# Block-diagonal inverses kept in DRAM as their 32x32 blocks, and the first weight splits and beta casts tied behind the input's work: one core of a Trainium2 chip

## The chip, the cores and the metric

The kernel runs on one core of a Trainium2 chip. The metric is the device time of one execution in microseconds (us); the time before is the median of three runs, 2675.2 us (2672.99 to 2676.81). TensorE is called PE, VectorE DVE, ScalarE ACT, GpSimd POOL and SyncE SP; SP only issues DMAs.

## What is computed

One layer of a hybrid decoder in float32 on 2048 prompt tokens (D = 1024) and 64 sample tokens (8 sequences of 8). Cut to what matters here:

```python
u = rms_norm(x, norm_pre)
z = einsum('btd,de->bte', u, w_in)           # w_in is 1024 x 8208
lru_x, lru_gate, gdn_qkv, gdn_gate, gdn_b, gdn_a, m_lru, m_gdn = split(z)
h, lru_h = rg_lru(conv(lru_x), ...)          # a linear recurrence
q, k, v = split(silu(conv(gdn_qkv)))         # 8 heads of 128
beta, g = sigmoid(gdn_b), -exp(A_log) * softplus(gdn_a + dt_bias)
# gated delta rule, chunk by chunk: M is strictly lower triangular
Tinv = inverse(I + M)                        # M from k, beta and g
u_, w_ = Tinv @ (v*beta), Tinv @ (k*beta*exp(gc))
...                                          # state S carried from chunk to chunk
merged = sigmoid(m_lru)*(lru_out @ w_br_lru) + sigmoid(m_gdn)*(gdn_out @ w_br_gdn)
x_new = x + rms_norm(merged @ w_out, norm_post)
```

The outputs are the new x of both batches and the states.

## The kernel before

The prompt is worked off in four **blocks** of 512 tokens (block 0 has the 64 sample tokens too). A block has these stages, each a Python loop that emits code: the K projections of the 8 heads with the Gram matrices of the chunks (`t_gram`), the LRU's projections with the inverses of the diagonal blocks beside them (`t_inv`), the gated-delta stage with Q, V and gate projections of the 8 heads (`t_inv2`, `t_q`, `t_v`, `t_chain`), the branch products and the output product. A projection (`proj`, lines 551, 553, 555) multiplies a 1024 x 128 slice of weights with the 512 tokens. Both are split into a rounded high and a low part (`split`, line 205 for the low part), so each product is three matmuls.

**Weights.** Block 0 reads each raw slice from `w_in` and the other matrices (`wload`: tiles `raws`, two buffers, and `raw`, pairs of slices), splits it on ACT (high part, line 143) and DVE (low part, line 205) into a tile `whl`, and stores the split pair to DRAM (`dW`, 1 MB, line 279). Blocks 1 to 3 read `dW` back (line 300). `whl` has three buffers, so in block 0 a split waits until an earlier pair's store has landed.

**The order of work.** PE executes in the order in which the code is emitted: a small planner (`Weave`) steps generators in between the matmuls of the projections. DVE, ACT, POOL and SP are ordered by the framework's scheduler. `keep_in_program_order(x)` ties an instruction behind what its engine was given before it in the program. All engines execute in order. SP's DMAs use eight semaphores in turn, so a DMA of SP waits until the eighth before it has landed.

**The start.** `u_load` and `u_norm` read the first 512 + 64 tokens and normalise them; `u_tile`, eight times, has PE transpose a slice (line 196), ACT round it (tile `a`, line 143) and DVE take the low part (line 358). Then `wst`, the beta and decay columns of `w_in`, is cast (lines 431 to 433) and multiplied first (line 192, 32 matmuls), then come the small constants and the projections.

**The inverses.** A chunk has 128 tokens; `t_gram` stores its 128 x 128 matrix to `dM`. `t_inv` loads the 32 x 32 diagonal blocks of all 32 chunks and heads, one block to a partition (`Mb`, line 836), inverts them on DVE and stores the inverse and its transpose into the diagonal blocks of `dD` and `dDT`, 128 x 128 for each chunk, by 8 DMAs of 32 partitions (lines 848, 849), whose pieces in DRAM have 128 bytes. The rest of `dD` and `dDT` is zero: `t_zero` writes it in block 0 by 16 DMAs of 256 KB (line 504, pieces of 512 bytes). For each head, `t_inv2` loads `dM` (`Mt`, line 990), `dD` (`Dn`, one buffer, line 991) and `dDT` (`R`, two buffers, line 992), 4 chunks of 128 x 128 each. PE multiplies `Mt` with `Dn`, and in three steps fills in the blocks of `R` above the diagonal, which DVE writes (line 1008). `R` is then what `t_chain` uses.

```python
SP.dma_start(Dn, dD[hc].rearrange("c j i -> j c i"))
SP.dma_start(R, dDT[hc].rearrange("c j i -> j c i"))
```

Of the kernel before, what the change touches and what calls it, by code (L numbers as in the profile page):

```python
# [22 lines left out]
F32 = mybir.dt.float32  # L23
# [11 lines left out]
NCH = TB // 128  # L35
SB = 0
NS = 64
H = 8
# [116 lines left out]
def body(ctx, tc, x_prompt, x_sample, state_lru_conv, state_lru_h, state_gdn_conv, state_gdn_S,  # L155
# [47 lines left out]
    def split(hi, lo, src, eng=None):  # L203
        r = A.activation(hi, src, AF.Copy)
        (eng or G).tensor_tensor(out=lo, in0=src, in1=hi.bitcast(F32), op=OP.subtract)  # L205
        return r
# [36 lines left out]
    wlast = [None]  # L243
# [37 lines left out]
    def wfetch(ahead):  # L281

        while wnext[0] < len(worder) and len(wready) < ahead:
            n = wnext[0]
            e = worder[n]
            place = wplace[key(e)]
            out = isinstance(e[1], tuple)
            hl = wtile()
            hi, lo = (hl[:, j].rearrange("p (k c) -> p k c", c=256 if out else 128) for j in range(2))
            if n < len(wplace):  # L290
                while lnext[0] < len(wplace) and lnext[0] <= n + (
                        2 if paired[0] <= lnext[0] < paired[1] else 1):
                    wload(lnext[0])
                    lnext[0] += 1
                wstore(1)
                wlast[0] = split(hi, lo, wraws[key(e)], V)
                wstores.append((place, hl))
            else:
                wstore()
                SP.dma_start(hl.bitcast(F32), dW[place])  # L300
            wready.append((hi, lo))
            wnext[0] += 1
# [81 lines left out]

    dk = dram.tile([H, 128, TB + NS], F32, name="dk")
    dM = dram.tile([H * NCH, 128, 128], F32, name="dM")
    dD = dram.tile([H * NCH, 128, 128], F32, name="dD")
    dDT = dram.tile([H * NCH, 128, 128], F32, name="dDT")
    dE = dram.tile([H, 128, TB], F32, name="dE")
    dtm = dram.tile([16, 128, TB + NS], F32, name="dtm")  # L390
    dgc = dram.tile([H * NCH, 128], F32, name="dgc")
# [20 lines left out]
    with tc.tile_pool(name="init", bufs=2, side="right") as ip:  # L412
        with tc.tile_pool(name="u0", bufs=1) as up:
            r0 = ip.tile([8, 128], F32, name="r0")
            SP.dma_start(r0, rows(norm_pre))
            xh = u_load(0, up)
            t = gtile()
            tr(t[:, :8], r0, ident[:8, :8])
            V.tensor_copy(npre, t[:, :8])
            wraw = ip.tile([128, 8, 16], F32, name="wraw", bufs=1)  # L420
            SP.dma_start(wraw, win[:, C_B:C_B + 16].rearrange("(k p) c -> p k c", p=128))
            u_norm(xh, up)
            for n in range(2):
                wload(n)
                lnext[0] += 1
            SP.dma_start(dtb, bass.AP(tensor=gdn_dt_bias.tensor, offset=gdn_dt_bias.offset, ap=[[0, 128], [1, 8]]))
            SP.dma_start(negA, bass.AP(tensor=gdn_A_log.tensor, offset=gdn_A_log.offset, ap=[[0, 128], [1, 8]]))
            u = [u_tile(xh, k) for k in range(8)]
            zz = ip.tile([128, 96], F32, name="zz", bufs=1)
            V.memset(zz, 0.0)  # L430
            V.tensor_copy(wst[:, 256:352], zz)
            V.tensor_copy(wst3[:, :, 0:16], wraw)
            V.tensor_tensor(out=wst3[:, :, 16:32], in0=wraw, in1=wst3[:, :, 0:16].bitcast(F32), op=OP.subtract)
            wfetch(2)
        G.affine_select(out=tri, in_=ones, pattern=[[1, 128]], compare_op=OP.is_ge, fill=0.0,
                        base=0, channel_multiplier=-1)
        G.affine_select(out=offm.rearrange("p (a b) -> p a b", b=32), in_=ones.rearrange("p (a b) -> p a b", b=32),
                        pattern=[[-32, 4], [0, 32]], compare_op=OP.is_ge, fill=0.0, base=-32,
                        channel_multiplier=1)
        V.tensor_scalar(offm, offm, -1.0, None, op0=OP.mult)  # L440

        blk = const.tile([64, 64], F32, name="blk")
        blk3 = blk.rearrange("p (a b) -> p a b", b=8)
        G.affine_select(out=blk3, in_=ones[:64, :64].rearrange("p (a b) -> p a b", b=8),
                        pattern=[[-8, 8], [0, 8]], compare_op=OP.is_ge, fill=0.0, base=0, channel_multiplier=1)
        G.affine_select(out=blk3, in_=blk3, pattern=[[8, 8], [0, 8]], compare_op=OP.is_ge, fill=0.0,
                        base=7, channel_multiplier=-1)
        tris = const.tile([64, 64], F32, name="tris")
        V.tensor_tensor(out=tris, in0=blk, in1=tri[:64, :64], op=OP.mult)
        negs = const.tile([64, 64], F32, name="negs")  # L450
        V.tensor_scalar(negs, tris, 1.0, BIG, op0=OP.subtract, op1=OP.mult)
        bsel = blk3[:, :, 0]
        G.memset(halog, 0.0)
        G.memset(halol, 0.0)
        G.memset(hlast, 0.0)
        tc.keep_in_program_order(A.activation(negA, negA, AF.Exp))
        V.tensor_scalar(negA, negA, -1.0, None, op0=OP.mult)
# [39 lines left out]
    def t_zero(pool):  # L497

        z = pool.tile([128, 4, 128], F32, name="lru7")
        G.memset(z, 0.0)  # L500
        for h in range(H):
            yield 7000.0
            for dst in (dD, dDT):
                SP.dma_start(dst[4 * h:4 * h + 4].rearrange("c i j -> i c j"), z)
        yield 7000.0
        SP.dma_start(dDs.rearrange("h i j -> i h j"),
                     z[:64].rearrange("p a b -> p (a b)").rearrange("p (a b) -> p a b", b=64))
        zeroed[0] = True
# [22 lines left out]
    for blkno in range(NBLK):  # L531
# [299 lines left out]
        def t_inv():  # L831
            yield lambda: all(kdone)
            Mb = kl.tile([128, 32, 32], F32, name="Mb", tag="Mbinv", bufs=1)
            for b in range(4):
                q = slice(32 * b, 32 * b + 32)
                SP.dma_start(Mb[q], dM[:, q, q])
            if sb:
                Mbs = kl.tile([64, 8, 8], F32, name="Mbs", tag="Mbinvs", bufs=1)
                for b in range(8):
                    q = slice(8 * b, 8 * b + 8)  # L840
                    SP.dma_start(Mbs[q], dMs[:, q, q])
            yield 3000.0
            r = []
            yield from tri_inverse(kl, 32, 128, Mb, "inv", r)
            yield lambda: zeroed[0]
            for b in range(4):
                q = slice(32 * b, 32 * b + 32)
                SP.dma_start(dD[:, q, q], r[0][q])
                SP.dma_start(dDT[:, q, q], r[1][q])
            yield T_IN  # L850
            invdone[0] = True
            if sb:
                r = []
                yield from tri_inverse(kl, 8, 64, Mbs, "invs", r)
                for b in range(8):
                    q = slice(8 * b, 8 * b + 8)
                    SP.dma_start(dDs[:, q, q], r[1][q])
# [121 lines left out]
        def h2t(nm, bufs=B2, shape=None):  # L979
            return h2.tile(shape or [128, NCH, 128], F32, name=nm, tag=nm, bufs=bufs)  # L980

        def t_inv2(h):

            d = st_[h]
            hc = slice(NCH * h, NCH * h + NCH)
            d["kT"] = h2t("kT", B2, [128, NB])
            SP.dma_start(d["kT"], dk[h, :, :NB])
            Mt, Dn = h2t("Mt", 1), h2t("Dn", 1)
            R = d["R"] = h2t("R")
            SP.dma_start(Mt, dM[hc].rearrange("c j i -> j c i"))  # L990
            SP.dma_start(Dn, dD[hc].rearrange("c j i -> j c i"))
            SP.dma_start(R, dDT[hc].rearrange("c j i -> j c i"))
            d["Ed"] = h2t("Ed")
            SP.dma_start(d["Ed"], dE[h].rearrange("p (c i) -> p c i", c=NCH))
            d["loaded"] = True
            yield T_I2 if h else T_I20
            yield lambda: invdone[0]
            t = g3()
            for c in range(NCH):
                mm(t[:, c], Mt[:, c], Dn[:, c])  # L1000
            V.tensor_tensor(out=Mt, in0=t, in1=bc(offm[:, None, :], [128, NCH, 128]), op=OP.mult)
            for a in (2, 1, 0):
                yield T_NEU
                rows, cols = slice(32 * a, 32 * a + 32), slice(32 * a + 32, 128)
                t = g3()
                for c in range(NCH):
                    mm(t[rows, c, cols], Mt[:, c, rows], R[:, c, cols], cost=54.0 * (3 - a))
                V.tensor_copy(R[rows, :, cols], t[rows, :, cols])
            d["inv"] = True
# [343 lines left out]
```

## Time and profile before

| | us |
|---|---|
| median of three runs | 2675.2 |
| lowest and highest of them | 2672.99, 2676.81 |
| profiled execution, its own time | 2665.83 |
| its span | 2664.1 |
| PE busy in the span | 2564.3 (96%) |
| mean granted clock of PE | 0.991 of full speed |

The profile is of one execution. "Busy" is time in which an engine executes; what an engine waits for is given as idle time with its releaser. The granted clock is a share of 2.4 GHz: a stretch at 1.00 ran at 2.4 GHz throughout, one at less ran at 1.2 GHz for some of its time. A view by stretches gives busy times, the clock and the share of time for which the 16 DMA engines were occupied (the modelled ends can make it slightly over 1).

### The profile page before, as it was taken

The numbers are of one execution on the slowest core, as the hardware profiler recorded it, in microseconds if no ns is written. First come the engines' busy times: TensorE is split into PE (matmuls) and PEld (weight loads), VectorE is DVE, ScalarE is ACT, GpSimd is POOL, SyncE is SP. The second block draws the span as 40 slices with busy tenths as digits, with TensorE's granted clock in tenths as the row PEclk, the third lists the DMA queues.
The fourth block names the chain that finished last, engine by engine and source line by source line (L and its number), as shares of the span: only waits on it lengthen the run. The fifth ranks groups of instructions, "written<-read, shape, count | busy, mean of one in ns | idle before, by whom it ended". The sixth has DMA issues, their size and how long they took to land.

```text
span 2664.1 us, 39927 instructions
## 1 busy us (share of the span) xinstructions
PE 2564.3 (96%) x15332; PEld 2232.2 (84%) x15332; DVE 1508.0 (57%) x3521; ACT 886.9 (33%) x1722; POOL 378.0 (14%) x364
## 2 busy tenths in 40 slices
PE   6988889998999999999999999999999999999999
PEld 5888888887999788888889888888889888888888
DVE  4668668776544457566513457566513457566512
ACT  5336533333333235333303235333303235333301
POOL 0220111001210111110200211110211211100210
PEclk9999999999999999999999999999999999999999
DMA  7997988788877786544466886644466886545465
GB/s 210 253 285 181 261 202 202 181 173 162 307 269 270 256 271 217 203 168 164 158 240 255 273 275 213 208 162 167 158 237 256 272 277 214 202 169 168 160 236 201
DMA packets 327897, 581.82 MB, mean 218 GB/s; under 512 B 70849, under 2 KB 236762, under 8 KB 282650
## 3 DMA queue, kind: packets, MB, share of 16 engines
q1 hardware_dynamic: 313882, 553.57, 66.6%
q10 hardware_dynamic: 13824, 25.70, 2.6%
q8 instruction: 121, 1.98, 0.3%
q14 instruction: 70, 0.57, 0.1%
HBM read 421.61 MB, written 157.59 MB: 217 GB/s over the span
## 4 chain that ended last, share of the span: by engine, by line
PE 77%; DMA 10%; DVE 6%; issue 2%; ACT 2%; SPq 1%; POOL 1%; ACTq 0%; POOLq 0%; DVEq 0%
PE mm L555 18%; PE mm L553 18%; PE mm L551 18%; PE g L192 8%; PE c L192 5%; PE g L196 2%; PE mm L1294 2%; PE mm L1296 2%; PE mm L1298 2%; DMA er<-dgc 2%; DMA raws<-in_w_in_dram 2%; DMA dW<-whl 2%; DVE cvy L582 1%; DVE whl L205 1%; DMA dE<-er 1%
## 5 line engine op out<-in xcount | busy, mean ns | idle before, releaser
L551 PE MATMUL mm<-a,whl 128*128 128x512 f32 (+2 forms) x2432 | 862.3, 355 | 15.6 <-ACT tmo L143 11.9
L555 PE MATMUL mm<-a,whl 128*128 128x512 f32 (+2 forms) x2432 | 867.4, 357 | 7.3 <-DVE whl L205 7.3
L553 PE MATMUL mm<-a,whl 128*128 128x512 f32 (+2 forms) x2432 | 862.1, 354 | 0.0
L551 PEld LDWEIGHTS mm<-a,whl 128*128 128x128 f32 x2432 | 464.7, 191 | 64.0 <-ACT tmo L143 12.7
L555 PEld LDWEIGHTS mm<-a,whl 128*128 128x128 f32 x2432 | 464.7, 191 | 60.8 <-DVE whl L205 8.3
L553 PEld LDWEIGHTS mm<-a,whl 128*128 128x128 f32 x2432 | 464.6, 191 | 45.5
L582 DVE SCALAR_TENSOR_TENSOR cvy<-cvr,cwg,cvy 128x512 f32<-128x512 f32 x288 | 217.4, 755 | 17.9 <-ACT cvy L143 12.5
L553 PE MATMUL mm<-a,whx 128*128 128x512 f32 x448 | 181.7, 406 | 0.0
L555 PE MATMUL mm<-a,whx 128*128 128x512 f32 x448 | 181.4, 405 | 0.0
L551 PE MATMUL mm<-a,whx 128*128 128x512 f32 x448 | 179.3, 400 | 0.0
L1232 DVE SCALAR_TENSOR_TENSOR pt<-tm,mm 128x512 f32<-128x512 f32 (+1 forms) x80 | 47.3, 592 | 180.7 <-PE mm L555 180.6
L143 ACT ACTIVATE cvr<-mm 128x512 f32<-128x512 f32 (+1 forms) x160 | 81.6, 510 | 186.9 <-PE mm L555 179.1
L1086 POOL TENSOR_TENSOR st<-st,mhalf 128x4 f32<-128x4 f32 x32 | 38.9, 1215 | 653.4 <-DVE st L1084 653.4
L1294 PE MATMUL mm<-whl,bt 128*128 128x256 f32 x448 | 126.2, 282 | 1.2 <-DVE y L1303 1.2
L1298 PE MATMUL mm<-whl,bt 128*128 128x256 f32 x448 | 126.2, 282 | 0.2 <-DVE yss L1272 0.2
L1296 PE MATMUL mm<-whl,bt 128*128 128x256 f32 x448 | 126.3, 282 | 0.0
L143 ACT ACTIVATE yv<-c 128x128 f32<-128x128 f32 x128 | 35.5, 277 | 245.9 <-PE c L192 245.4
L143 ACT ACTIVATE th<-cvy 128x512 f32<-128x512 f32 (+1 forms) x96 | 61.9, 645 | 156.4 <-DVE cvy L582 130.9
L555 PE MATMUL mm<-gp,whl 128*128 128x512 f32 (+2 forms) x296 | 104.2, 352 | 0.0
L551 PE MATMUL mm<-gp,whl 128*128 128x512 f32 (+2 forms) x296 | 104.1, 352 | 0.0
L553 PE MATMUL mm<-gp,whl 128*128 128x512 f32 (+2 forms) x296 | 104.0, 351 | 0.0
L551 PEld LDWEIGHTS mm<-a,whx 128*128 128x128 f32 x448 | 84.5, 189 | 17.6
(341 smaller groups left out, 4476.1 us busy)
## 6 DMA issues: line engine op xcount, KB each, us to landing
whl<-dW SPq DMA_DIRECT2D x199, 1024.0 KB
dW<-whl SPq DMA_DIRECT2D x88, 1024.0 KB
whx<-dW SPq DMA_DIRECT2D x65, 1024.0 KB
raws<-in_w_in_dram SPq DMA_DIRECT2D x33, 512.0 KB
raw<-in_w_in_dram SPq DMA_DIRECT2D x15, 1024.0 KB
dtm<-tmo ACTq DMA_DIRECT2D x48, 256.0 KB
tm<-dtm SPq DMA_DIRECT2D x48, 256.0 KB
ux<-in_x_prompt_dram SPq DMA_DIRECT2D x16, 512.0 KB
```

Source lines behind the costliest of these rows:

```text
L143: r = f(*args, **kw)
L192: T.matmul(out, a, b, start=start, stop=stop)
L196: T.transpose(out, in_, idn)
L551: T.matmul(ps[:, :n], wh, mh[:, c0:c0 + n], start=k == 0, stop=False)
L553: T.matmul(ps[:, :n], wh, ml[:, c0:c0 + n], start=False, stop=False)
L555: T.matmul(ps[:, :n], lo[:, k, :], mh[:, c0:c0 + n], start=False, stop=k == 7)
L582: V.scalar_tensor_tensor(out=y[:, :TB], in0=raw[:, i:i + TB], scalar=cw[:, i, ti:ti + 1], in1=y[:, :TB], op0=OP.mult, op1=OP.add)
L1086: G.tensor_tensor(out=st[:, 3], in0=st[:, 2], in1=mhalf[:, :NCH], op=OP.pow)
L1232: proj(mov, lambda ps, c0, n: V.scalar_tensor_tensor(out=t_[:, c0:c0 + n], in0=x[:, c0:c0 + n], scalar=1.0, in1=ps[:, :n], op0=OP.add, op1 ...
L1294: T.matmul(ps[:, :256], mh[:, cs], wh[:, k % 4], start=k == 0, stop=False)
L1296: T.matmul(ps[:, :256], mh[:, cs], wl[:, k % 4], start=False, stop=False)
L1298: T.matmul(ps[:, :256], ml[:, cs], wh[:, k % 4], start=False, stop=k == 7)
```

## The change

```diff
@@ wfetch
                 wlast[0] = split(hi, lo, wraws[key(e)], V)
+                if n < 4:
+                    tc.keep_in_program_order(wlast[0])
@@
-    dD = dram.tile([H * NCH, 128, 128], F32, name="dD")
-    dDT = dram.tile([H * NCH, 128, 128], F32, name="dDT")
+    dD = dram.tile([4, H * NCH, 32, 32], F32, name="dD")
+    dDT = dram.tile([4, H * NCH, 32, 32], F32, name="dDT")
@@ the start
-            V.memset(zz, 0.0)
+            tc.keep_in_program_order(V.memset(zz, 0.0))
             V.tensor_copy(wst[:, 256:352], zz)
-            V.tensor_copy(wst3[:, :, 0:16], wraw)
+            tc.keep_in_program_order(V.tensor_copy(wst3[:, :, 0:16], wraw))
@@ t_zero
-        G.memset(z, 0.0)
-        for h in range(H):
-            yield 7000.0
-            for dst in (dD, dDT):
-                SP.dma_start(dst[4 * h:4 * h + 4].rearrange("c i j -> i c j"), z)
+        G.memset(z[:64], 0.0)
@@ t_inv
-            for b in range(4):
-                q = slice(32 * b, 32 * b + 32)
-                SP.dma_start(dD[:, q, q], r[0][q])
-                SP.dma_start(dDT[:, q, q], r[1][q])
+            for dst, m in ((dD, r[0]), (dDT, r[1])):
+                SP.dma_start(dst.rearrange("b n i j -> (b n) i j"), m)
@@ before t_inv2, once for each block
+        blkd = []
+        for i in range(3):
+            blkd.append(h2.tile([128, NCH, 128], F32, name=f"blkd{i}"))
+            G.memset(blkd[i], 0.0)
@@ t_inv2
-            Mt, Dn = h2t("Mt", 1), h2t("Dn", 1)
-            R = d["R"] = h2t("R")
+            Mt, Dn = h2t("Mt", 1), blkd[2]
+            R = d["R"] = blkd[h % 2]
             SP.dma_start(Mt, dM[hc].rearrange("c j i -> j c i"))
-            SP.dma_start(Dn, dD[hc].rearrange("c j i -> j c i"))
-            SP.dma_start(R, dDT[hc].rearrange("c j i -> j c i"))
+            for b in range(4):
+                q = slice(32 * b, 32 * b + 32)
+                SP.dma_start(Dn[q, :, q], dD[b, hc].rearrange("c i j -> i c j"))
+                SP.dma_start(R[q, :, q], dDT[b, hc].rearrange("c i j -> i c j"))
```

`dD` and `dDT` now hold only the diagonal blocks. The 16 DMAs of zeros are gone; each block's 8 stores of inverses become 2, of 128 partitions with pieces of 4 KB; each head's two loads become 8 of 32 partitions (pieces of 128 bytes) into tiles that POOL has set to zero once in the block. The first four splits on ACT, and on DVE the zero columns and the first cast of `wst`, are tied behind what their engines were given before.

ACT at the start: `whl<-raws` is the high part of a weight split, `a<-g,npre` the rounding of a transposed slice of the input, 512 columns for the prompt and 64 for the samples. Two pieces of the difference:

```order
 L143 ACTIVATE ux_216<-ux_216,urr 128x1024
-L143 ACTIVATE whl<-raws 128x1024
-L143 ACTIVATE a<-g,npre 128x512
-L143 ACTIVATE a<-g,npre 128x64
-L143 ACTIVATE whl<-raws 128x1024
-L143 ACTIVATE a<-g,npre 128x512
-L143 ACTIVATE a<-g,npre 128x64
-L143 ACTIVATE negA<-negA 128x8
-L143 ACTIVATE a<-g,npre 128x512
-L143 ACTIVATE a<-g,npre 128x64
-L143 ACTIVATE whl<-raws 128x1024
```

```order
+L143 ACTIVATE a<-g,npre 128x512
+L143 ACTIVATE a<-g,npre 128x64
+L143 ACTIVATE whl<-raws 128x1024 x2
+L143 ACTIVATE negA<-negA 128x8
 L143 ACTIVATE zr<-mm 32x256
 L143 ACTIVATE zr<-mm 32x320
```

The three splits that stood between the roundings are gone from there; two stand behind the eighth pair, and the third and the fourth further down, behind the Tanh of the first K projection (`th`). On DVE, the low parts of the first two and the casts of `wst` stand behind the eight low parts of the input too.

SP a little later, first before, then changed: `raws` and `raw` are raw weights, `dW` a store of a split pair, `dD<-lru` and `dDT<-lru` the first zeros.

```order
L473 DMA er<-in_state_lru_h_dram 64x128
L265 DMA raws<-in_w_in_dram 128x8x128
L271 DMA raw<-in_w_in_dram 128x8x256
L279 DMA dW_80<-whl 128x2048
L271 DMA raw<-in_w_in_dram 128x8x256
L279 DMA dW_81<-whl 128x2048
L279 DMA dW_82<-whl 128x2048
L504 DMA dD<-lru_870 128x4x128
L504 DMA dDT<-lru_870 128x4x128
```

```order
L475 DMA er<-in_state_lru_h_dram 64x128
L271 DMA raw<-in_w_in_dram 128x8x256 x2
L265 DMA raws<-in_w_in_dram 128x8x128 x2
L279 DMA dW_80<-whl 128x2048
L279 DMA dW_81<-whl 128x2048
L504 DMA dDs<-lru_870 64x8x64
L271 DMA raw<-in_w_in_dram 128x8x256
```

The third raw slice, which was loaded among the constants, now comes with the fourth, behind the loads of slices 4 to 7. Further on, two more `raws`, of the slices that are used around 310 us, stand some 20 and 35 DMAs behind these rows; before, they came behind the inverses' stores.

POOL and SP at the start of the gated-delta stage of block 1, changed (before, the three rows of `blkd` were not there, and SP had one `Dn` and one `R` in place of the eight loads). `lru<-lru,lhz` is the LRU's gating, `hlast` the last column of a recurrence.

```order
L907 COPY hlast<-lru_11324 128x1
L981 MEMSET blkd_11377 128x512
L981 MEMSET blkd_11379 128x512
L935 TENSOR_TENSOR lru_10927<-lru_10927,lhz 128x512
L981 MEMSET blkd_11381 128x512
L935 TENSOR_TENSOR lru_10931<-lru_10931,lhz 128x512
```

```order
L991 DMA Mt<-dM 128x4x128
L994 DMA blkd_11381<-dD 32x4x32
L995 DMA blkd_11377<-dDT 32x4x32
L994 DMA blkd_11381<-dD 32x4x32
L995 DMA blkd_11377<-dDT 32x4x32
L994 DMA blkd_11381<-dD 32x4x32
L995 DMA blkd_11377<-dDT 32x4x32
L994 DMA blkd_11381<-dD 32x4x32
L995 DMA blkd_11377<-dDT 32x4x32
L997 DMA Ed<-dE 128x512
L302 DMA whl<-dW_119 128x2048
```

`blkd_11381` is the tile that `Dn` is in; its memset stands third, behind one LRU gating, and the first of SP's eight loads waits for it.

## Rows read from the trace of the kernel before

**Rows 1.** Busy time of each engine, from the page.

```profile
PE 2564.3 (96%) x15332; PEld 2232.2 (84%) x15332; DVE 1508.0 (57%) x3521; ACT 886.9 (33%) x1722; POOL 378.0 (14%) x364
```

**Rows 2.** Busy time by stretches: two of block 0, one of block 1.

```profile
core 0: us, PE busy (x) PEld busy (x) DVE busy (x) ACT busy (x) POOL busy (x), PEclk, DMA share, GB/s
...
160.00:180.00 20.00, 14.48 (x92) 14.07 (x90) 11.04 (x28) 6.75 (x12) 6.44 (x6) 0.83 0.97 337
...
280.00:300.00 20.00, 16.54 (x108) 16.13 (x108) 9.59 (x19) 11.06 (x22) 2.08 (x2) 0.83 1.02 284
...
1080.00:1120.00 40.00, 40.00 (x235) 32.49 (x234) 24.62 (x48) 8.28 (x16) 5.94 (x6) 1.00 0.65 224
```

**Rows 3.** Waits in 45:372: waiter, awaited, us in total, times, longest.

```profile
PE mm L551 <- ACT tmo L143: 11.9, 4, 5.5
...
PE g L192 <- DMA Dn<-dD: 6.8, 1, 6.8
...
ACT whl L143 <- DMA dW<-whl: 61.0, 14, 11.3
```

**Rows 4.** The chain that ended last, three pieces: start, us, what.

```profile
152.14 12.52 DMA er<-dgc
...
261.87 6.54 SPq L848
...
273.99 0.91 SPq L279
```

**Rows 5.** Timeline of the start: start, us, engine, line, operation, tiles [idle before].

```profile
16.06 1.81 PE L196 MATMUL g<-ident,ux 128*128 128x128 f32 x6 [5.00 <-ACT ux L143]
...
18.35 1.06 ACT L143 ACTIVATE whl<-raws 128x1024 fp32r<-128x1024 f32 x1 [2.34 <-DMA raws<-in_w_in_dram]
...
28.97 1.06 ACT L143 ACTIVATE whl<-raws 128x1024 fp32r<-128x1024 f32 x1 [3.98 <-DMA raws<-in_w_in_dram]
...
30.05 1.23 DVE L205 TENSOR_TENSOR whl<-raws,whl 128x1024 fp32r<-128x1024 f32 x1 [4.67 <-ACT whl L143]
...
32.00 2.75 PE L196 MATMUL g<-ident,ux 64*128 64x64 f32 x10 [4.98 <-DVE a L358]
...
34.97 1.71 PE L196 MATMUL g<-ident,ux 64*128 64x64 f32 x6 [0.22 <-DVE a L358]
...
36.42 0.89 ACT L143 ACTIVATE a<-g,npre 128x512 fp32r<-128x512 f32 x2 [0.73 <-PE g L196]
...
36.61 6.42 PE L192 MATMUL mm<-a,wst 128*128 128x256 f32 x32
```

**Rows 6.** Timeline of ACT around the second projection's end.

```profile
57.51 0.69 ACT L143 ACTIVATE th<-cvy 128x576 f32<-128x576 f32 x1
...
58.62 0.44 ACT L143 ACTIVATE tmo<-mm 128x320 f32<-128x320 f32 x1 [0.16 <-PE mm L555]
```

**Rows 7.** DMA queue (packets, MB, share of 16 engines): 1192.6:1193.9, 1035:1039; total of 64:69.

```profile
q1 hardware_dynamic: 513, 0.26, 66.7%
...
q1 hardware_dynamic: 4440, 0.56, 91.1%
...
DMA packets 902, 1.92 MB, mean 384 GB/s; under 512 B 73, under 2 KB 684, under 8 KB 715
```

**Rows 8.** Timeline of SP, POOL and PE at the gated-delta stage of block 1.

```profile
1083.60 0.50 SPq L991 DMA_DIRECT2D Dn<-dD  x1
...
1085.27 2.54 POOL L939 TENSOR_TENSOR lru<-lru,lhz 128x512 f32<-128x512 f32 x2 [0.48 <-DVE lhz L934]
...
1091.05 1.05 PE L192 MATMUL g<-Dn,Mt 128*128 128x128 f32 x8
```

**Rows 9.** Timeline, prices: a memset of POOL; a small load alone and its user.

```profile
36.23 0.52 POOL L500 MEMSET lru<- 128x512 f32 x1 [20.89 <-PE g L196]
...
0.81 0.41 SPq L415 DMA_DIRECT2D r<-in_norm_pre_dram  x1
...
2.34 0.24 PE L196 MATMUL g<-ident,r 8*128 8x8 f32 x1 [2.34 <-DMA r<-in_norm_pre_dram]
```

## The prediction

> **What bounds the kernel now.** I read the page's busy times first, then the stretches, the waits, and the chain. PE is busy for 96% of the span [rows 1], so what can be won is its 100 us of idle time and what its lower clock costs. The stretches tell where that lies. Block 1 shows none: PE is busy for 40.00 of 40 us at full clock, and the DMA engines are occupied for only 0.65 of the time [rows 2]. Block 0 is different. From 160 to 180 us PE is busy for 14.48 us, with the DMA engines at 0.97; from 280 to 300 for 16.54 us, with DMA at 1.02. Both stretches have a granted clock of 0.83 [rows 2]: PE ran at 1.2 instead of 2.4 GHz for a third of the stretch, behind a stall, and lost 0.17 x 20 = 3.4 us by it. So a change is worth something only where it acts in block 0, and costs something wherever PE must wait that did not.
>
> The waits say what block 0 is short of. PE waits for ACT, but ACT waits 61.0 us, in 14 waits of up to 11.3, for the store of an earlier weight pair to land, to reuse its tile [rows 3]. The chain agrees: a load of `er` takes 12.52 us to land, where a small load alone takes 1.53 from issue to use (0.81 to 2.34) [rows 4, 9]. From 261.87 to 273.99 the chain runs through SP itself, which issues the stores of the inverses [rows 4]. Block 0 is bound by turns by the DMA queue and by PE.
>
> **The change part by part.**
>
> *The start.* ACT executes in order and sat 2.34 us and 3.98 us before a raw weight had landed, with the input's rounding behind it; PE then waited 4.98 us for the input's slices [rows 5]. The ties take both waits out. Without them a slice takes 1.49 us (two between 32.00 and 34.97), so eight from 16.06 end at 27.98. Behind them come the last rounding, 0.89, the first split, 1.06 on ACT and 1.23 on DVE [rows 5], and the subtraction of the casts, 0.2 by its columns (128 against 1024): the first `wst` matmul starts at 31.4 instead of 36.61, 5.2 us earlier. The next link comes late in exchange: the third split now stands behind `th`, which ends at 57.51 + 0.69 - 5.2 = 53.0. With 1.06 and 1.23 its low part is there at 55.3, where the third projection could start at 58.62 - 5.2 = 53.4 [rows 5, 6] and needs it 0.3 later: 1.6 us are given back. Net **-3.6 us**; bounds -5.2, and 0 if the later loads of slices 3 and 4 (issued behind 2 MB of others) hold PE up for the rest. Those 2 MB take 5.2 us at 384 GB/s [rows 7] and start some 25 us before they are needed, so I take the value near the first bound.
>
> *The zeros.* One 256 KB transfer in 512-byte pieces occupies all DMA engines for 0.667 x 1.3 = 0.87 us [rows 7]. Sixteen are 13.9 us, gone from block 0's first half. Two raw slices that were loaded later now stand in that half: 0.5 MB each in twice as many 512-byte pieces, so 1.7 us each at the least, and at most the 4.0 us that ACT waited for one; at 3 each they take 6 back. The remaining 8 us count only where the queue is what PE waits for; as PE is idle for a quarter of such a stretch and busy in others [rows 2], I take half: **-4 us**, bounds 0 and -13.9.
>
> *The stores of the inverses.* Eight DMAs of 1024 pieces of 128 bytes are 8192 pieces; 4440 take 4 us at 91.1% [rows 7], so they occupy the DMA engines for 6.7 us. The same megabyte at 384 GB/s takes 2.7 [rows 7]. SP, which was held from 261.87 to 273.99 [rows 4], issues two DMAs instead, at 0.5 each [rows 8]. Between the 4.0 us that the engines gain and the 11 us of SP's chain I take **-8 us**: the weights' stores stood right behind on SP (273.99), and ACT waits for just those. In blocks 1 to 3 PE has no idle time that this could take: 0.
>
> *The clock.* If the two stretches of rows 2 lose most of their idle time, their 2 x 3.4 us come back as well. I take **-3 us**, bounds 0 and -6.8.
>
> *The loads of each head.* They keep the number of pieces (512) with a quarter of the bytes. In the running stage `Dn` is issued as soon as its tile is free, a whole head ahead; that covers six more issues. At the stage's start there is no such cover. In block 1 `Dn` was issued at 1083.60 and used at 1091.05 [rows 8]. Now it waits for POOL's third memset. Two of 0.52 us [rows 9] come before an LRU gating and fill its idle 0.48, so that starts at 1085.83 and ends at 1087.10; the third ends at 1087.62. Of SP's eight DMAs the seventh is the last for `Dn`. At 0.5 us each it is issued at 1090.6, and lands 1.53 later [rows 9] at 1092.2: PE waits 1.1 us. For three blocks **+3.3 us**; bounds 0 (the memsets find POOL free earlier) and the serial loading below. In block 0 PE already waits 6.8 us for `Dn` [rows 3]. There the loads get shorter but SP must issue more of them, with at most eight in flight: 0, bounds -6.8 and +3.
>
> On this point the trace is weighed against a rule. Rows 8 and 9 say that small loads overlap: one issue takes 0.5 us and its landing 1.53. The Trainium skill (DMA: Bandwidth & Descriptors, Rules for kernel authors) says to coalesce small transfers, as one under 64 KB is mostly overhead, and its fit in "Anatomy of one DMA" gives 2.0 us plus the bytes at 436 GB/s. These loads have 16 KB. By that fit, one after another, the seventh would land 14.3 us behind 1087.6, PE would wait 10.8 us in each block, and the sum would come out some 29 us higher. No row shows one load of SP waiting for the one before it.
>
> **The sum** is -3.6 - 4 - 8 - 3 + 3.3 = -15.3 us. The profiled execution's own time, 2665.83 us, would be 2650.5. The median of the runs, 2675.2, lies 9.4 above that execution, and all three runs lie within 2.3 of it; I set the sum against the median: 2659.9, in round figures **2660 us**. With the bounds of the queue's terms this case holds 2650 to 2669.
>
> **The rivals.** *Block 0 was held by its DMA work throughout.* Then the whole 13.9 us of zeros, SP's 11 and both clock terms (6.8) come off, with the start's 5.2: -36.9 + 3.3, **2642 us**. For it speaks ACT's 61.0 us [rows 3]; against it, that PE is busy for 72 to 83% of the worst stretches all the same [rows 2], and that two raw slices move into the relieved half.
>
> *The stalls are order, not volume.* ACT, DVE and SP execute in order, and the scheduler has set block 0's order anew. If `er` and the splits wait for one another in new places, the queue's 12 us come back as other waits, and the start's gain ends at the first of them: what stays is within 0.2% of the median, which is about what a measurement of this kernel can tell from no change, say **2673 us**. For it speaks that PE's wait for ACT's `tmo` (5.5 us) is an in-order wait behind `er`; against it, that `er` itself waited for its load [rows 3, 4].
>
> *Slower: the loads of a head go one after another.* If each of SP's eight ends before the next one counts, seven take 7 x 1.53 = 10.7 us from 1087.6 [rows 9], `Dn` lands at 1098.3, and PE waits 7.3 us. A stall of that size was followed by a lower clock, worth 3.4 us [rows 2]. So a block loses 10.7, three lose 32, and with -18.6 from the other terms the time is **2689 us**. It decides from 6.2 us for each block. Against it: SP issued `Dn` 7.4 us before its use, with other loads before and behind it, and PE did not wait.
>
> That the change does not do what it says can nearly be left out: the order of the changed kernel has the splits behind the roundings and 16 DMAs fewer of zeros.
>
> **How the numbers follow.** Forecast 0.50 (2660), all of block 0's DMA 0.22 (2642), no difference 0.17 (2673), slower 0.11 (2689). Faster by over 0.2% (below 2669.8): the first two, 0.72; within 0.2%: 0.17; slower by over 0.2% (above 2680.6): 0.11. The range goes from 2636, the second case with 6 us more where block 0's own `Dn` wait ends too, to 2681, past the third; it leaves out the serial case and what is left of the others' edges.
>
> **What would show it.** Right: the first `wst` matmul near 31.4 us; ACT's wait for the weights' stores well under 61.0; no SP chain at the stores; clock dips gone near 160 and 280; a PE wait of about 1 us for `Dn` in blocks 1 to 3 and none elsewhere there. Wrong: `wst` near 36; idle time of PE in block 0 as before with other releasers; waits for `Dn` over 6 us in the later blocks.

## The result, and the profile after

| | before | changed |
|---|---|---|
| median, us | 2674.09 (four runs, 2668.21 to 2676.81) | 2643.91 (four runs, 2642.73 to 2649.12) |
| ratio, 95% interval | 1 | 0.9894, 0.9872 to 0.9916 |
| profiled execution, its own time | 2665.83 | 2642.97 |
| its span | 2664.1 | 2641.3 |

The change takes 28 us off (0.0106 x 2674): the direction of the forecast, 2660, and nearly twice its 15 us. The time lies in the stated range and next to the first rival's 2642.

The page of the changed kernel, its busy line and its DMA line, with the DMA line of the kernel before behind them:

```profile
PE 2559.1 (97%) x15332; PEld 2227.2 (84%) x15332; DVE 1507.8 (57%) x3521; ACT 885.7 (34%) x1722; POOL 382.4 (14%) x376
...
DMA packets 290394, 565.07 MB, mean 214 GB/s; under 512 B 73281, under 2 KB 198234, under 8 KB 245146
```

```profile
DMA packets 327897, 581.82 MB, mean 218 GB/s; under 512 B 70849, under 2 KB 236762, under 8 KB 282650
```

PE is busy 5.2 us less than in [rows 1], and the span is 22.8 us shorter: most of what went is idle time. The DMA engines move 16.8 MB less: 4.2 are the zeros (16 DMAs of 256 KB), the other 12.6 are the smaller loads of the heads, over the four blocks. Stretches of the changed kernel (columns as in [rows 2]):

```profile
110.00:130.00 20.00, 12.62 (x83) 12.62 (x84) 9.87 (x28) 5.48 (x12) 4.93 (x7) 0.74 0.99 318
160.00:180.00 20.00, 20.00 (x151) 19.60 (x151) 11.60 (x36) 6.72 (x15) 3.44 (x6) 1.00 0.91 249
220.00:240.00 20.00, 9.84 (x60) 9.54 (x59) 16.24 (x58) 9.41 (x17) 2.06 (x2) 0.83 0.93 221
280.00:300.00 20.00, 20.00 (x152) 20.00 (x151) 18.71 (x48) 16.82 (x30) 2.18 (x3) 1.00 0.64 253
```

The two stretches of [rows 2] that had stalls are full and at full clock now; the work that stood in them comes earlier and takes 11.7 and 14.5 us in place of 20. But there are other stalls: around 120 and 230 us PE is busy for 63% and 49% of the time, at clocks of 0.74 and 0.83. Three of the waits in 45:372:

```profile
ACT whl L143 <- DMA dW<-whl: 18.4, 7, 7.7
...
PE mm L549 <- ACT cvy L143: 13.4, 3, 9.2
...
PE g L192 <- DMA blkd<-dDT: 8.2, 1, 8.2
```

The wait of 9.2 us is the stall near 120. The one near 230 is a wait of 5.9 us for ACT's `lt` and one of 4.3 for a split (their rows stand below, with the stores); that of 8.2 is the head loads of block 0. ACT's wait for the weights' stores fell from 61.0 us in 14 waits [rows 3] to 18.4 in 7. The start, PE, DVE and ACT together:

```profile
13.95 11.33 PE L196 MATMUL g<-ident,ux 128*128 128x128 f32 x37 [2.21 <-ACT ux L143]
...
28.49 5.92 PE L192 MATMUL mm<-a,wst 128*128 128x256 f32 x32 [3.21 <-DVE wst L435]
...
26.93 1.22 DVE L205 TENSOR_TENSOR whl<-raws,whl 128x1024 fp32r<-128x1024 f32 x1
28.06 0.28 DVE L435 TENSOR_TENSOR wst<-wraw,wst 128x128 fp32r<-128x128 f32 x1
...
25.64 2.00 ACT L143 ACTIVATE whl<-raws 128x1024 fp32r<-128x1024 f32 x2
...
53.19 1.06 ACT L143 ACTIVATE whl<-raws 128x1024 fp32r<-128x1024 f32 x1 [2.09 <-DMA dW<-whl]
```

The first `wst` matmul starts at 28.49 instead of 36.61. The start of block 1's gated-delta stage, POOL, SP and PE, against [rows 8]:

```profile
1057.54 0.99 POOL L981 MEMSET blkd<- 128x512 f32 x2
1058.49 1.28 POOL L935 TENSOR_TENSOR lru<-lru,lhz 128x512 f32<-128x512 f32 x1
1059.72 0.53 POOL L981 MEMSET blkd<- 128x512 f32 x1
...
1060.27 0.32 SPq L994 DMA_DIRECT2D blkd<-dD  x1
1060.68 0.38 SPq L995 DMA_DIRECT2D blkd<-dDT  x1
...
1063.01 0.43 SPq L994 DMA_DIRECT2D blkd<-dD  x1
...
1064.87 1.13 PE L192 MATMUL g<-blkd,Mt 128*128 128x128 f32 x8 [0.84 <-DMA blkd<-dD]
```

The third memset ends at 1060.25, SP issues the first load at 1060.27 and the seventh at 1063.01, and PE waits 0.84 us, as the forecast had it step by step. PE's waits for a load of `dD`, one in each of blocks 1 to 3:

```profile
PE g L192 <- DMA blkd<-dD: 2.5, 3, 0.9
```

Where the time came from is read best from the start of the same PE instruction in both traces (PE executes 15332 in the same order). By the clock of the kernel before, the changed kernel is ahead by 12.3 us at 100, by 0.6 at 120, 12.7 at 180, 24.4 at 240, 12.0 at 260, 27.2 at 310 and 27.7 at 614, and at the end by 22.9; about 1 us is lost at the start of the gated-delta stage in each of blocks 1 to 3, and the other 2 in smaller steps. All is won in block 0, with two setbacks on the way, at the stalls near 120 and 230 of the rows above.

### The profile page after: what moved, and what is told of

It reads as the page before. It is cut to its first block, busy times and chain, and to the rows that moved or that the text cites. A ratio compares the mean times of both kernels' runs of the same rounds, so it can differ in the third digit from the quotient of the medians.

```text
span 2641.3 us, 40215 instructions
## 1 busy us (share of the span) xinstructions
PE 2559.1 (97%) x15332; PEld 2227.2 (84%) x15332; DVE 1507.8 (57%) x3521; ACT 885.7 (34%) x1722; POOL 382.4 (14%) x376
## 4 chain that ended last, share of the span: by engine, by line
PE 77%; DMA 6%; DVE 6%; ACT 2%; POOL 1%; issue 1%; SPq 1%; ACTq 0%; POOLq 0%; DVEq 0%
PE mm L553 19%; PE mm L551 18%; PE mm L549 18%; PE g L192 8%; PE c L192 5%; PE g L196 2%; PE mm L1297 2%; PE mm L1299 2%; PE mm L1301 2%; DVE cvy L580 1%; DMA dW<-whl 1%; DMA er<-dgc 1%; DVE whl L205 1%; DMA dE<-er 1%; DVE lru L905 0%
## 5 line engine op out<-in xcount | busy, mean ns | idle before, releaser
L580 DVE SCALAR_TENSOR_TENSOR cvy<-cvr,cwg,cvy 128x512 f32<-128x512 f32 x288 | 216.7, 753 | 18.6 <-ACT cvy L143 13.3
L192 PEld LDWEIGHTS g<-blkd,Mt 128*32 128x32 f32 (+1 forms) x1024 | 78.2, 132 | 45.6 <-issue 31.4
L192 PE MATMUL g<-blkd,Mt 128*128 128x128 f32 (+3 forms) x1024 | 96.6, 238 | 10.7 <-DMA blkd<-dDT 8.2
L553 PE MATMUL mm<-gp,whl 128*128 128x512 f32 (+2 forms) x296 | 104.2, 352 | 0.0
L549 PE MATMUL mm<-gp,whl 128*128 128x512 f32 (+2 forms) x296 | 104.1, 352 | 0.0
```

The source lines that it names most:

```text
L192: T.matmul(out, a, b, start=start, stop=stop)
L549: T.matmul(ps[:, :n], wh, mh[:, c0:c0 + n], start=k == 0, stop=False)
L553: T.matmul(ps[:, :n], lo[:, k, :], mh[:, c0:c0 + n], start=False, stop=k == 7)
L580: V.scalar_tensor_tensor(out=y[:, :TB], in0=raw[:, i:i + TB], scalar=cw[:, i, ti:ti + 1], in1=y[:, :TB], op0=OP.mult, op1=OP.add)
```

## The experiments

Each kernel ran in rounds beside the kernel before on the same chip. One per mille is 2.7 us. The difference of two ratios of this table is uncertain by some 5 to 7 us.

| kernel | us | ratio, interval | ACT's wait for `dW`, 45:372 |
|---|---|---|---|
| changed, again | 2641.45 | 0.9897, 0.9881 to 0.9914 | 16.4 |
| compact blocks alone | 2649.0 | 0.9927, 0.9911 to 0.9943 | 14.7 |
| ties alone | 2666.23 | 1.0001, 0.9985 to 1.0017 | 59.1 |
| without the splits' ties | 2647.75 | 0.9941, 0.9922 to 0.9960 | 10.7 |
| without the beta ties | 2640.22 | 0.9904, 0.9888 to 0.9919 | 13.9 |
| old stores | 2640.98 | 0.9897, 0.9879 to 0.9915 | 6.3 |
| zeros back | 2661.97 | 0.9981, 0.9968 to 0.9994 | 49.0 |
| zeros and old stores | 2660.96 | 0.9974, 0.9961 to 0.9986 | 57.7 |
| zeros of 2 KB | 2650.0 | 0.9937, 0.9921 to 0.9952 | 42.1 |
| zeros from ACT | 2651.98 | 0.9951, 0.9934 to 0.9968 | 17.3 |
| zeros of 2 KB from ACT | 2645.73 | 0.9924, 0.9905 to 0.9942 | 15.4 |
| zeros in block 1 | 2638.6 | 0.9902, 0.9882 to 0.9921 | 19.6 |
| `Dn` set to zero first | 2638.58 | 0.9898, 0.9880 to 0.9916 | 16.7 |
| two early loads put back | 2636.78 | 0.9884, 0.9866 to 0.9903 | 19.1 |
| both of these | 2635.92 | 0.9888, 0.9867 to 0.9910 | 13.3 |

**The two halves apart.** Compact blocks without the three ties, and the ties without compact blocks; the changed kernel beside them.

> The changed kernel once more, on the chip on which its parts run. 2644 us, about 30 us under the kernel before. Nothing is decided by it alone: it is the other end of the sums below.

> The compact blocks alone, without the three ties. Forecast as recorded: zeros -4, stores -8, clock -3, later blocks +3.3, so 11.7 us under before, about 2662. Volume (block 0 was held by its DMA work, and the forecast halved its terms): zeros and stores in full, about 24 under, 2650; ACT's wait for the weights' stores falls from 61 us to under 25 with the first wst matmul still at 36.6. Ties (the start was worth more than forecast and all of it is kept to the end): at most 12 under, 2662 or more. Order (what the scheduler does with the rest decides): the gains of this run and of the ties alone miss the whole 30 us by over 8 us.

> The three ties alone, with the zeros and the stores of before. The first wst matmul starts near 28.5 us instead of 36.6 by every theory. Forecast as recorded: 3.6 us under before, 2670. Volume: the queue that holds block 0 takes nearly all of it back, 0 to 4 under, and ACT's wait for the weights' stores stays at 50 us or more. Ties: 8 or more under, 2666 or less, and the gain is still there at 600 us.

The compact blocks alone gain 0.73%, 19 us, the ties alone nothing, both together 1.03%, 27 us. So the ties are worth 8 us (0.30%), but only when the zeros are gone. For the compact half volume (24 under) is nearer than the forecast (11.7), and ACT's wait falls as volume had it. The ties alone show what becomes of a gain ahead of the queue. The chain of waits and ACT in that kernel, from 36 us on:

```profile
36.95 5.03 SPq L279
42.03 14.31 DMA dW<-whl
...
56.86 1.06 ACT L143 ACTIVATE whl<-raws 128x1024 fp32r<-128x1024 f32 x1 [5.72 <-DMA dW<-whl]
```

Its `wst` starts at 28.60 and PE is 8.2 us ahead of the kernel before at 40 us, 2.9 at 80, and 0.9 behind at 100: a store of a weight pair takes 14.31 us to land, and the fourth split, whose turn on ACT comes early now, waits 5.72 us for it (2.09 in the changed kernel, whose row stands above). What was won ahead of the queue is waited for in it.

**Which tie.** The changed kernel without the one, and without the other.

```diff
-                if n < 4:
-                    tc.keep_in_program_order(wlast[0])
```

```diff
-            tc.keep_in_program_order(V.memset(zz, 0.0))
+            V.memset(zz, 0.0)
-            tc.keep_in_program_order(V.tensor_copy(wst3[:, :, 0:16], wraw))
+            V.tensor_copy(wst3[:, :, 0:16], wraw)
```

> The changed kernel without the ties of the four splits; those of the beta casts stay. Without the beta ties it ran as fast as with them. If the splits' ties carry all that the ties are worth: as the compact blocks alone, 2649, with the first wst matmul near 36 us. If either pair of ties is enough: 2641, with wst near 29.

> The changed kernel without the two ties of the beta casts; the ties of the splits stay. The trace shows PE's transposes starting 2.1 us earlier and DVE no longer waiting 3.3 us for the beta columns. If that wait is worth its time: transposes start at 16.0 instead of 13.9 and the kernel takes 2 to 3 us more, 2644. If the input's slices only wait for ACT (as forecast, which gave these ties 0.2 us): within 1 us of the changed kernel, 2641.

The splits' ties carry it: without them the ratio is 0.9941, 0.44% (12 us) above the changed kernel's, as with the compact blocks alone, and ACT sits before the raw weights as in [rows 5] (the kernel without the splits' ties):

```profile
18.28 1.06 ACT L143 ACTIVATE whl<-raws 128x1024 fp32r<-128x1024 f32 x1 [4.83 <-DMA raws<-in_w_in_dram]
22.21 1.06 ACT L143 ACTIVATE whl<-raws 128x1024 fp32r<-128x1024 f32 x1 [2.09 <-DMA raws<-in_w_in_dram]
28.59 1.06 ACT L143 ACTIVATE whl<-raws 128x1024 fp32r<-128x1024 f32 x1 [2.64 <-DMA raws<-in_w_in_dram]
```

The beta ties cost as much as they give, as far as the ratios can tell (0.9904 against 0.9897). PE without them:

```profile
17.24 1.81 PE L196 MATMUL g<-ident,ux 128*128 128x128 f32 x6 [5.81 <-ACT ux L143]
...
28.50 5.63 PE L192 MATMUL mm<-a,wst 128*128 128x256 f32 x32
```

The transposes start 3.3 us later than with the ties, but the casts are done by then, and `wst` starts at 28.50 without a wait. With the ties PE is through earlier and waits 3.21 us for the casts behind the eighth slice: 28.49.

**The stores.** The changed kernel with the 8 stores of 128-byte pieces, and later the same with the zeros as well. (Of the edit, the stores; the matrices in DRAM are 128 x 128 again, and the eight loads of a head read their diagonal blocks.)

```diff
-            for dst, m in ((dD, r[0]), (dDT, r[1])):
-                SP.dma_start(dst.rearrange("b n i j -> (b n) i j"), m)
+            for b in range(4):
+                q = slice(32 * b, 32 * b + 32)
+                SP.dma_start(dD[:, q, q], r[0][q])
+                SP.dma_start(dDT[:, q, q], r[1][q])
```

> The changed kernel with one part undone: the inverses are stored as before by 8 DMAs with pieces of 128 bytes, into 128 x 128 matrices of which only the diagonal blocks are written and read. No zeros, same loads. Forecast as recorded: 8 us more than the changed kernel, 2652. Volume alone: the 4 us of DMA time that the pieces cost, 2648. Order or cover: within 2 us of the changed kernel, and a chain through SP at the stores that costs PE nothing.

> Zeros and old stores together: the 16 DMAs of 256 KB, as in the run with the zeros on SP, and the inverses stored by 8 DMAs with pieces of 128 bytes. The zeros alone gave 2662. Forecast's 8 us for the stores, true only in the full queue: 2668 to 2670, as the kernel before. The stores cost nothing there either: 2662 within 2 us.

No cost that can be told in either: 0.9897 against 0.9897, and 0.9974 against 0.9981. The forecast's 8 us (0.30%) fit neither; the second pair leaves room for 3 us at most. SP is held all the same, here in the kernel with old stores:

```profile
242.31 0.31 SPq L846 DMA_DIRECT2D dD<-invT  x1
243.47 1.68 SPq L847 DMA_DIRECT2D dDT<-invTT  x1
245.20 4.29 SPq L846 DMA_DIRECT2D dD<-invT  x1
...
254.25 2.03 SPq L279 DMA_DIRECT2D dW<-whl  x2
```

SP is held for 11.9 us (242.31 to 254.25), as it was before, and the weights' stores stand behind. But PE's waits of 220:300 in this kernel are those of the changed one (this kernel first, then the changed one):

```profile
ACT whl L143 <- DMA dW<-whl: 6.1, 1, 6.1
PE g L192 <- ACT lt L143: 5.3, 1, 5.3
PE mm L553 <- DVE whl L205: 4.7, 2, 4.5
```

```profile
ACT whl L143 <- DMA dW<-whl: 12.8, 3, 7.7
...
PE g L192 <- ACT lt L143: 5.9, 1, 5.9
...
PE mm L553 <- DVE whl L205: 4.3, 1, 4.3
```

ACT even waits less for the weights' stores with the old stores: neither of PE's two waits is longer by more than 0.4 us.

**The zeros: bytes, places or order.** 16 DMAs back into the changed kernel, into two matrices that nothing reads, with 256 KB and then with 2 KB each; both kernels have the same order on every engine.

```diff
-        G.memset(z[:64], 0.0)
+        G.memset(z, 0.0)
+        for h in range(H):
+            yield 7000.0
+            for dst in (dZ, dZT):
+                SP.dma_start(dst[4 * h:4 * h + 4].rearrange("c i j -> i c j"), z)
```

With 2 KB, the last line is:

```diff
+                SP.dma_start(dst[4 * h:4 * h + 4, :1].rearrange("c i j -> i c j"), z[:1])
```

> The changed kernel with the 16 DMAs of zeros back (256 KB each, pieces of 512 bytes, into two matrices that nothing reads). Forecast as recorded: 4 us more than the changed kernel, 2645. Volume: the compact blocks without ties gained 19 us and the stores none of it, so the zeros cost 15 to 22, 2657 to 2663, and ACT's wait for the weights' stores is back above 45 us. Order: it is the places that the 16 DMAs take on SP, with what waits behind them, so this run and the next cost the same.

> As the run before, in the same order on every engine, but each of the 16 DMAs stores one row of four matrices, 2 KB instead of 256. Forecast: 2641, no cost (16 issues of half a us on an engine that only issues). Volume: within 3 us of the changed kernel, and ACT's wait for the weights' stores stays below 25 us. Order: as dear as the full zeros, 2657 or more; between them, the order's share is this run's distance from the changed kernel.

The zeros cost 0.84%, 22 us, as much as the whole gain of the compact half (19 us, without the ties). Between the theories: 0.40% (11 us) stay with 2 KB, and 0.44% (12 us) are bytes, close to the 13.9 us for which they occupy the DMA engines. With 2 KB the stores of the weights still come late: ACT waits for them for 42.1 us against 16.4. The 16 rows on SP also gave the rows behind them a new order (PE's stays); what of the 11 us is the places and what that order is not told apart. The run with zeros and old stores above differs from the ties alone only in the heads' loads and in that its zeros go to matrices which nothing reads; it is 0.27% (7 us, uncertain by 5) faster. So something beside zeros, stores and ties gains; the 12.6 MB that the loads no longer move and the order that came with them are candidates, and no run has the new loads by themselves.

So the order was held in the next pair: the zeros issued by ACT, which leaves SP, DVE and PE in the order of the changed kernel. Against the kernel with the zeros back:

```diff
-                SP.dma_start(dst[4 * h:4 * h + 4].rearrange("c i j -> i c j"), z)
+                A.dma_start(dst[4 * h:4 * h + 4].rearrange("c i j -> i c j"), z)
```

> The 16 zero DMAs of 256 KB are back, but issued by ACT, not SP: SP, DVE and PE keep the order of the changed kernel (SP and POOL but for one row each), and ACT keeps its own with 16 issues more. So the 4 MB are priced with the order held. Zeros on SP cost 21 us, of which 9 were there with 2 KB in place of 256. Volume: the 12 us that are left (13.9 us of DMA time) come back here, 2651 to 2656, and ACT's wait for the weights' stores rises from 16 to 30 us or more. Order: it is SP's order and its eight semaphores that cost, so this run stays within 3 us of the changed kernel, 2641 to 2644.

> As the run before, with 2 KB in each DMA of zeros: what 16 more issues on ACT cost by themselves. Both theories: within 2 us of the changed kernel, 2641. Were it dearer than that, the run before would have to be read against this one.

0.54% (14 us) dearer than the changed kernel, and 0.27% (7 us) than the same with 2 KB: a second price for the bytes, 7 us, that agrees with 12 within its uncertainty. Two expectations missed. ACT's wait for the weights' stores did not rise (17.3), and 16 tiny DMAs on ACT cost 0.27%, barely more than can be told. What the 16 tiny ones cost is not shown. One candidate: in the trace ACT's DMAs signal on the same eight semaphores as SP's, so the zeros take turns there from either engine. ACT pays at its own DMAs; a `th` of the kernel with 256 KB, and its chain:

```profile
85.44 0.68 ACT L143 ACTIVATE th<-cvy 128x576 f32<-128x576 f32 x1 [4.96 <-DMA dZ<-lru]
...
103.85 19.08 DMA dZT<-lru
122.95 10.92 DMA dZT<-lru
```

**The same bytes in block 1.**

```diff
+        if blkno == 1:
+            W.add(t_zlate(lruP_), 20000.0)
```

(`t_zlate` is the loop of zeros, issued by SP.)

> The changed kernel with the 16 DMAs of zeros in block 1's first projections, issued by SP; the order of all else is kept. In block 1 PE is busy all the time and the DMA engines 0.65 of it. Volume as forecast: DMA time has a price only in block 0, so 4 MB cost nothing here, 2641 within 2 us, and PE's shift against the changed kernel does not move between 600 and 1200 us. If the chip charges for the transfers wherever they are: 4 to 14 us more.

No cost that can be told: 0.9902 against 0.9897, 1 us with an uncertainty of 7. PE's lead over the changed kernel (its second run) does not fall either: 6.3 us at 600, 8.9 at 1200. The stretch in which they run, here and in the changed kernel's second run:

```profile
780.00:840.00 60.00, 59.98 (x459) 57.38 (x458) 27.16 (x58) 20.56 (x53) 3.27 (x6) 1.00 0.95 318
```

```profile
780.00:840.00 60.00, 57.53 (x459) 56.50 (x458) 28.27 (x53) 18.86 (x48) 2.74 (x5) 0.97 0.71 253
```

The DMA engines go from 0.71 to 0.95 and PE is busy throughout. A high DMA share alone is no bound. In block 0 it goes with ACT's waits for stores before it can reuse a tile; that these waits make the difference is argued from the rows, no run takes them away by themselves.

**The loads of a head, and two early loads.** First the order of the three memsets; then the two raw slices that the changed kernel loads early (SP at 86.43 and 116.89) tied to their place, after which they are loaded at 290.51 and 292.84; then both.

```diff
             blkd.append(h2.tile([128, NCH, 128], F32, name=f"blkd{i}"))
+        for i in (2, 0, 1):
             G.memset(blkd[i], 0.0)
```

In `wload`:

```diff
-            SP.dma_start(raw, src[:, c:c + 128].rearrange("(k p) c -> p k c", p=128))
+            dl = SP.dma_start(raw, src[:, c:c + 128].rearrange("(k p) c -> p k c", p=128))
+            if paired[1] <= n < paired[1] + 2:
+                tc.keep_in_program_order(dl)
```

> The changed kernel with one order changed: the tile of `Dn` is set to zero first of the three, not last, so its memset stands before the LRU's gating on POOL. If POOL's third memset is what holds the first loads of blocks 1 to 3 (as forecast), PE's waits of about 1 us for `Dn` are gone there and the time is 3 us lower, 2638. If the eight loads themselves are late (SP issues them one by one), the waits stay at 1 us each and the time at 2641.

> The changed kernel with one order changed: the two raw slices that SP loads early (at 86 and 117 us, used around 310) are tied to their place in the program, some 70 DMAs later, behind the stores of the inverses, as before the change. All else keeps its order but for a few weight stores that step over their places. Forecast as recorded: the early loads take 6 us of the relieved first half, so without them the time is lower, 2635. If the 9 us of order that came with the 2 KB zeros are the late loads of these slices (there they were back in their old place): 5 to 9 us more, 2646 to 2650. If it is SP's places: within 2 us of the changed kernel, 2641.

> Dn's tile set to zero first, and the two early raw loads tied back to their place. The first alone gave 2638.6, the second alone 2636.8, the changed kernel 2641.5. If both gains are real and lie in different blocks (the memset's 3 us in blocks 1 to 3, the loads' up to 5 in block 0): 2634, and PE has no wait for Dn behind 700 us. If the loads' gain was chance: 2638.

With `Dn` first, PE has no wait in front of these matmuls (block 1's row; the changed kernel's has 0.84):

```profile
1060.25 1.05 PE L192 MATMUL g<-blkd,Mt 128*128 128x128 f32 x8
```

That is shown for the waits (2.5 us in three, gone). In the time 2 to 3 us can't be resolved: 2638.6 against 2641.5 by the medians, 0.9898 against 0.9897 by the ratios. The early loads are not what the 11 us are: put back, the kernel is no slower (0.9884). Whether they cost the forecast's 6 us or nothing stays open, as 0.13% (3.5 us) is less than the uncertainty. Both edits together have the lowest median, 2635.92, 30 us under the kernel before; over the changed kernel the gain isn't resolved.

## Why the prediction was right in direction and wrong in size

- **The zeros, -4: measured -22.** This is the step that failed most. The forecast had the bytes at 13.9 us, took 6 off for two early loads and halved the rest, since PE is busy in part of such a stretch. The runs give 7 and 12 us for the bytes, so half or more of 13.9 counts and not half of what the loads leave; and 11 us come with 16 places on SP and the order behind them, to which the forecast gave no price. ACT's 61.0 us of waiting in [rows 3] were the sign that block 0 waited for its stores again and again; with the zeros back the wait is 49.0.
- **The stores of the inverses, -8: measured 0**, within the uncertainty, with and without the zeros in the queue. The step went wrong where it took a chain through SP [rows 4] for a price. It showed that what ended last was waiting for SP; with it shortened, PE waits in that stretch for `lt` and for a split, as long as with the old stores.
- **The start, -3.6: right in kind, larger.** `wst` came at 28.49, not 31.4. The forecast priced the ties of the beta casts at nothing and let the slices begin at 16.06 as before; they begin at 13.95. DVE had waited for the beta columns, with a scaling of the input behind it (the kernel before):

```profile
13.87 0.23 DVE L432 CAST wst<-wraw 128x128 fp32r<-128x128 f32 x1 [3.33 <-DMA wraw<-in_w_in_dram]
...
15.37 0.75 DVE L345 TENSOR_SCALAR ux<-ux,urr 64x1024 f32<-64x1024 f32 x1 [0.76 <-POOL urr L341]
```

  Behind the slices `wst` waits 3.21 us where the forecast had 3.4 of rounding, split and casts, nearly as said; that wait is what the beta ties give back, so that they come out at nothing. About 1.3 us are lost at the third split, as forecast (1.6): PE is 8.1 us ahead at `wst` and 6.8 at 60, and between them it waits 0.6 us for the split's high part and 0.8 for its low part. What reaches the end is 8 us (0.30%), or nothing with the zeros in the queue: the forecast's sum of separate terms has no place for that.
- **The clock, -3: not there.** The mean granted clock is 0.991 before and after. The dips of [rows 2] went, and others came with the other stalls (0.74 at 110 to 130).
- **`Dn` in blocks 1 to 3, +3.3: right**, in its place and its steps: 0.84 us in block 1 where 1.1 was forecast, 2.5 in the three, and the memset is the cause. The slower rival is excluded with it: seven loads of 16 KB take 4.6 us from the first issue to use (1060.27 to 1064.87), not 10.7; they overlap, issued 0.46 us apart. The Trainium skill (DMA: Bandwidth & Descriptors, "Anatomy of one DMA") gives its fit for one DMA on the path of GpSimd, and these loads are issued by SP; that seven of them would take 14.3 us was the forecast's estimate from it, one after another, and this trace does not bear it out.
- **The sum.** The measured prices do not add up as the forecast's terms do, since they depend on what else is there. Along one row of kernels, each against the one before it: ties alone 0, with the new loads (zeros and old stores) -7, with the new stores (zeros back) +2, without the zeros (changed) -22: together -27, which is the 0.9897 of the second measurement. Along the other: compact blocks -19, ties -8. So the loads, which the forecast had at +3.3, may have gained more than PE's 2.5 us of waits cost; this is not shown. The rival "block 0 held by its DMA work throughout" came within 2 us of the time by luck: its 11 us of SP and 6.8 of clock were not there, and terms that it did not have made up for them. The rival "order, not volume" was right in that bytes are about half of the zeros' price, and wrong in that the rest came as a gain. The forecast's own bound of 2669 is 1 us above what its zeros at 0 and its stores at 4.0 give (2667.9).

## What to carry to other kernels

Where an engine waits again and again for its own stores to land, price a transfer that shares their queue at half to nearly all of its DMA time (7 and 12 of 13.9 us here) and its places too, and expect a gain ahead of that queue to be lost in it until the queue is relieved. A stretch of the chain that runs through an issuing engine is not yet a price: ask what ends last without it. The same bytes in a stage that is full of PE's work cost nothing that could be told here.

## What the runs showed that was not expected

A DMA share near 1 says little of the bytes that move: at 0.99 the changed kernel moved 318 GB/s in 110:130, at 0.93 only 221 in 220:240. Around the latter a store of 1 MB took 19.43 us to land and a raw load 11.88 (its chain):

```profile
205.03 19.43 DMA dW<-whl
...
226.50 11.88 DMA raw<-in_w_in_dram
```

And a stall of PE that goes can come back as another. The stall near 120 in the changed kernel, and what stands in its place without the beta ties:

```profile
117.38 0.63 PE L549 MATMUL mm<-a,whl 128*128 128x320 f32 x1 [9.19 <-ACT cvy L143]
```

```profile
PE mm L549 <- ACT cvs L143: 6.2, 1, 6.2
```

Without these ties PE is 10.2 us ahead of the changed kernel at 120, but it then stands for 6.2 us 24 matmuls further on, until 118.36 of its own time, and at 125 the lead is 1.8: PE waits for ACT in both.
